# Expert-mixing loop of an encoder block: multiplications by the gate in turn with the value chunks, the gate table in two buffers of 4 chunks instead of one of 8, and the gathered block's work spread to the last chunk

## The chip, the cores and the metric

The kernel runs on one core of a Trainium2 chip. Five engines share the core's on-chip memory: TensorE (PE in the profile, with its weight loads as PEld), VectorE (DVE), ScalarE (ACT), GpSimd (POOL), and SyncE (SP), which here only issues DMAs. Each engine works through its own queue strictly in order and waits on semaphores that other engines or DMAs raise. The metric is the device time of one execution in microseconds (us), median of several runs; lower is better.

## The reference, cut to what matters

One encoder layer over 512 tokens of width 1024 in float32: a mixing part (attention and a gated recurrence), then a PEER layer, then a gated embedding. The part that the change is about is the PEER layer, a retrieval over 16384 experts, each of one neuron:

```python
# ht: 512 tokens; idx, g: for every token 8 heads x 16 chosen experts and their softmax weights
ue = jnp.take(u, ib, axis=0)                    # rows of u of the chosen experts
a = jnp.einsum('thkd,td->thk', ue, xb)
w = jax.nn.gelu(a) * gb
ve = jnp.take(v, ib, axis=0)                    # rows of v
out = jnp.einsum('thk,thkd->td', w, ve)
```

After it come a residual add, an RMSNorm, a product with `ple_gate` under a sigmoid, a product with `p @ ple_proj`, and the last residual add.

## The kernel before, in words

Float32 matrices are split into a high and a low part of a rounded format (`split`: ACT copies the high part, line 139, DVE subtracts to get the low part, line 140), and every product is three matmuls (`mm3`, lines 133 to 136).

The PEER layer is computed in two ways. For tokens 128 to 511 (384 tokens) it is dense: all 16384 experts, in 128 chunks of 128 experts. For each chunk `dense_a` computes gelu(u · h) as a tile `ge` of 128 experts x 384 tokens (24 matmuls of 384 columns into `pa`, gelu on ACT). The weights of the chosen experts stand in a dense table in DRAM, `gdram` (zero where an expert was not chosen), which `build` has written. Later the chunk's `ge` is multiplied by its part of the table, split into `w_h` and `w_l`, and multiplied with the chunk's 128 rows of v (`w_mm`, 18 matmuls of 512 columns into the six accumulators `po`). For tokens 0 to 127 (block 0) it is sparse: GpSimd gathers, by indirect DMA, one row of u per token and slot (`gu`, 128 slots), DVE multiplies and sums it (line 889), then one row of v per slot (`gv`), which DVE adds into `acc` (line 898).

The order of the work: 62 of the 128 chunks have their `ge` computed while the table is still being built, and are spilled to DRAM (`adram`); the other 66 ("fresh") are computed inside the last loop. That loop (line 1014) runs over the 128 chunks; spilled and fresh ones alternate almost one to one (`chunk_order`). In each round `w_prep` does this:

- if the chunk is the first of a group of `GC` = 8, it loads the table for 8 chunks into `gchg` (line 988, 1536 KB, in rows of `GC` x `GB` x 4 = 1024 bytes). There is one such buffer (`B_GC` = 1), so the load waits until the last multiplication of the group before is done;
- it loads the chunk of v (`v_raw`, line 990, 512 KB, 3 buffers) and splits it into `v_h` and `v_l` (4 buffers each);
- for a spilled chunk it loads `ges` (line 996, 192 KB, 4 buffers), for a fresh one it takes the next `ge` (a ring of `PRE` = 8 buffers);
- DVE multiplies `ge` by the table (line 999, "the multiplication"), and the product is split into `w_h` and `w_l`.

Then `next_a` computes further fresh chunks (u is loaded on line 713, split into `u_h`, `u_l`), `w_mm` follows, and `gathers` traces as many gather steps as a pace asks for: the steps on u reach their last slot at round 110 (`IT1` - `UEND`), those on v at round 118 (`IT1`). All DVE steps of the gathers are tied behind the round's multiplication (`issue_after(dve.ins)`). The program is traced in this order, but a scheduler fixes the order of each queue at compile time from priorities and estimated times; `issue_after` adds an edge that it has to keep. So multiplications may stand in DVE's queue well ahead of the v splits of earlier chunks, if their inputs are estimated to be there.

At round 118 the pools of the u side are closed, the residual rows `X` are loaded back, `PJ` = p · ple_proj is computed, `acc` is added to `X[0]` (line 1058), and block 0 is finished as far as its first gate tile (`norm_T1` and `gate(0, 0)`, lines 1086 and 1087). The matmuls of the last 4 chunks (`LASTN`) are kept back and run block by block after the loop (line 1088), so that each block's norm can begin while the next block's matmuls run. Then come the other 15 gate tiles (24 matmuls of 256 columns each) and the output.

Of the kernel before, what the change touches and what calls it, by code (L numbers as in the profile page):

```python
# [27 lines left out]

C_ID, C_IOTA, C_COS, C_SIN, C_RST = 0, 128, 256, 384, 512
C_END = C_RST + 2 * T  # L30
# [4 lines left out]
LASTN = 4  # L35
GC = 8
B_GC = 1
HPU = 300
# [9 lines left out]
NTB = TD // GB  # L48
PRE = 8
SP = 62  # L50
# [8 lines left out]
HPW = 1  # L59
IT1 = 118  # L60
WLAG = 4
VLEAD = 0
# [23 lines left out]
def const_arrays():  # L86
    c = np.zeros((128, C_END), np.float32)
    c[:, C_ID:C_ID + 128] = np.eye(128, dtype=np.float32)
    c[:, C_IOTA:C_IOTA + 128] = np.arange(128, dtype=np.float32)[None]
    t = np.arange(T)  # L90
    row, col = (t // 64).astype(np.float32), (t % 64).astype(np.float32)
    inv = np.float32(10000.0) ** (-np.arange(16, dtype=np.float32) / np.float32(16))
    ang = np.stack([row[:, None] * inv, col[:, None] * inv], axis=1).astype(np.float32)
    for off, fn in ((C_COS, np.cos), (C_SIN, np.sin)):
        c[:, off:off + 128] = fn(ang).astype(np.float32).reshape(NT, 128, 32).transpose(1, 0, 2).reshape(128, 128)
    rst = np.ones((8, 128), np.float32)
    rst[:, 0] = 0.0
    c[:, C_RST:C_END] = rst.reshape(-1)[None]
# [27 lines left out]
def body(nc, tc, I, out, taps=None, stop=99):  # L126
# [17 lines left out]
    with contextlib.ExitStack() as top:  # L144
        glob = top.enter_context(tc.tile_pool(name="glob", bufs=1))
        cst = glob.tile([128, C_END], F32, name="cst")
        ident = cst[:, C_ID:C_ID + 128]
# [48 lines left out]
        if True:  # L196
# [17 lines left out]
            with tc.tile_pool(name="n1", side="right", bufs=1) as n1:  # L214
                ss = n1.tile([128, NT], F32, name="ss1")
                x1 = [n1.tile([128, D], F32, name=f"x1_{tb}") for tb in range(NT)]
                sq = n1.tile([128, D], F32, name="sq1")
                DM.dma_start(x1[0], I["x"][0:128, :])
                DM.dma_start(cst[:, 0:C_COS], I["cst"][:, 0:C_COS])
# [7 lines left out]
                DM.dma_start(cst[:, C_COS:C_END], I["cst"][:, C_COS:C_END])  # L227
# [105 lines left out]
            def hgrn_head(h):  # L333
# [4 lines left out]
                fl = "p a t -> p (a t)"  # L338
                V.tensor_tensor_scan(SC.rearrange(fl), cst[:, C_RST:C_END], LF.rearrange(fl), 0.0, OP.mult, OP.add)
                S4 = SC.rearrange("p a (c j) -> p a c j", c=4)  # L340
# [143 lines left out]
            for tb in range(NT):  # L484
                for (src, dst, H, o, gg) in ((aq[:, tb, :], qr, 8, 0, qn_g), (akv[:, tb, 0:128], kr, 2, 8, kn_g)):
# [7 lines left out]
                    co, si = [cst[:, off + 32 * tb:off + 32 * tb + 32].rearrange("p (a i) -> p a i", a=2)[:, None]  # L493
                              .to_broadcast([128, H, 2, 16]) for off in (C_COS, C_SIN)]
# [157 lines left out]
        h2n = pp.tile([128, D], F32, name="h2n")  # L652
        v8s = [pp.tile([128, 16, 16], F32, name=f"v8_{tb}") for tb in range(NT)]
        i8s = [pp.tile([128, 16, 16], U32, name=f"i8_{tb}") for tb in range(NT)]
        with s5:
# [101 lines left out]
def peer(nc, tc, I, out, xd, cst, gains, norm_T1, rstd_of, split, mm3, tap, stop, pp, ha, la, h2n, v8s, i8s, st, top,  # L757
# [8 lines left out]
    if True:  # L766
# [112 lines left out]
        un, vn = I["peer_u"], I["peer_v"]  # L879

        def gather(src, k, tag):
            t = gt.tile([128, D], F32, name=tag, tag=tag)
# [90 lines left out]
        if stop <= 6:  # L973
            return

        vp = ys.enter_context(tc.tile_pool(name="vstr", side="right", bufs=2, reuse_waits="tile"))
        pso = ys.enter_context(tc.psum_pool(name="pso", side="right", bufs=1, reuse_waits="tile"))
        po = [[pso.tile([128, 512], F32, name=f"po{tc_}{n}") for n in range(2)] for tc_ in range(3)]
        gch = {}
        N0 = na  # L980
        def w_prep(it):
            c = it
            spilled = it in spidx
# [8 lines left out]
            vl = vp.tile([128, D], F32R, name="v_l", tag="v_l", bufs=B_VS)  # L992
            split(vr, vh, vl)
            if spilled:
                ge = vp.tile([128, TD], F32, name="ges", tag="ges", bufs=B_GE)
                DM.dma_start(ge, ad[spidx[c]])
            else:
                ge = pend.pop(0)
            mi = V.tensor_tensor(ge.rearrange("p (b t) -> p b t", t=GB), ge.rearrange("p (b t) -> p b t", t=GB),  # L999
                                 gch[key][:, :, c % GC, :], op=OP.mult)  # L1000
            wh = vp.tile([128, TD], F32R, name="w_h", tag="w_h", bufs=B_W)
# [12 lines left out]
        for it in range(128):  # L1014
# [7 lines left out]
            else:  # L1022
                last.append((it, ops))
            if it < IT1:
                if it >= G0:
                    gathers(GW + (it + 1 - G0) * (128 + WLAG - GW) / (IT1 - UEND - G0), VLEAD + (it + 1 - G0) * 128 / (IT1 - G0), ops[0], ops[5])
            if it == IT1:
                gathers(999, 999, ops[0], ops[5])
                ul_st.close()
# [7 lines left out]
                with tc.tile_pool(name="ple1a", side="left", **LR) as pa:  # L1037
# [7 lines left out]
                    for n in range(2):  # L1045
# [6 lines left out]
                        for tb in range(NT):  # L1052
# [4 lines left out]
                            S.activation(PJ[tb][:, 512 * n:512 * n + 512], pj, AF.Copy)  # L1057
                V.tensor_tensor(X[0], X[0], acc, op=OP.add)
                pe2 = [e1.enter_context(tc.tile_pool(name="ple2", side="left", **LR))]
# [25 lines left out]
                wg0 = load_wg(0)  # L1085
                norm_T1(pe2[0], ps1, "p1", X[0], 2, h3h, h3l, "n3", 0, B_XN)
                gate(0, 0, *wg0, ps1, "p1")
        for tb in range(3):
            for it, ops in last:
                w_mm(it, tb, ops)  # L1090
            for n in range(2):
                xs = X[tb + TB0][:, 512 * n:512 * n + 512]
                V.tensor_tensor(xs, xs, po[tb][n], op=OP.add)
            norm_T1(pe2[0], ps1, "p1", X[tb + TB0], 2, h3h, h3l, "n3", tb + TB0, B_XN)
        ys.close()
        with contextlib.ExitStack() as e2:
            pe2.append(e2.enter_context(tc.tile_pool(name="ple3", side="right", **LR)))
            ps = e2.enter_context(tc.psum_pool(name="psp", side="right", bufs=4, reuse_waits="tile"))
            for n in range(4):
                w = wg0 if n == 0 else load_wg(n)  # L1100
                for tb in range(1 if n == 0 else 0, NT):
                    gate(tb, n, *w, ps, "pg2")
# [58 lines left out]
```

## Time and profile before

| | us |
|---|---|
| median of 3 runs | 1895.51 |
| lowest and highest of them | 1892.5, 1896.64 |
| the profiled execution, as timed | 1892.72 |
| its span, first to last instruction | 1890.9 |
| PE busy | 1811.2 (96%) |
| PE weight loads busy | 1618.7 (86%) |
| DVE busy | 1394.3 (74%) |
| ACT busy | 901.9 (48%) |
| POOL busy | 385.4 (20%) |

The span is what the profile's own clock shows; 1.8 us of the profiled execution lie around it. "PEclk" is the share of full speed that TensorE's clock was granted. In waits, "A <- B: x, n, y" says that engine A's instruction stood idle x us in n times, the longest y us, and B ended that. In groups, "xN | busy, mean ns | idle before" says how many instructions there were, how long they were busy, how long one took on average, and how long the engine had been idle just before them. Busy times of matmuls are modelled ends: a matmul shown with 0.39 us is followed by the next one 0.23 us later.

### The profile page before, as it was taken

The page shows a single profiled execution, that of the slowest core. Times are in us where ns is not written, and L with a number is a line of the kernel's source. Part 1 is how long each engine was busy: PE and PEld are TensorE (multiplying, and loading weights), DVE is VectorE, ACT ScalarE, POOL GpSimd, SP SyncE. Part 2 cuts the span into 40 slices and gives each one's busy share as a digit, 9 for nine tenths or more (in the row PEclk, how much of TensorE's full clock was granted, in tenths as well). Part 3 has the DMA queues.
Part 4 walks back from the last instruction along what each step waited for, and adds up shares of the span by engine and source line. Part 5 has one row for each costly group of instructions (what it writes and reads, how often), then busy time and mean ns, then how long its engine had stood idle before and what let it go on. Part 6 is the DMA issues. An engine that isn't in the chain of part 4 may idle for free.

```text
span 1890.9 us, 27215 instructions
## 1 busy us (share of the span) xinstructions
PE 1811.2 (96%) x9989; PEld 1618.7 (86%) x9989; DVE 1394.3 (74%) x2844; ACT 901.9 (48%) x1561; POOL 385.4 (20%) x260
## 2 busy tenths in 40 slices
PE   6999999999998999998999999999998988999998
PEld 5997887888787999998998888888887877888888
DVE  3689777535798999998656787887877666757464
ACT  5745656532433566975894333333332323333452
POOL 0000000000000222425001345554444333211000
PEclk9999999999999999999999999999999999999999
DMA  4212100333421678888659999999987877776512
GB/s 163 79 46 84 51 12 16 129 102 100 163 83 50 229 260 330 299 291 318 265 201 328 343 352 339 352 334 345 347 300 276 301 267 281 273 250 213 207 59 87
DMA packets 137975, 402.95 MB, mean 213 GB/s; under 512 B 13297, under 2 KB 56049, under 8 KB 136177
## 3 DMA queue, kind: packets, MB, share of 16 engines
q1 hardware_dynamic: 100976, 266.98, 40.3%
q0 software_dynamic: 36864, 134.23, 19.7%
q8 instruction: 78, 1.28, 0.3%
q14 instruction: 57, 0.46, 0.1%
HBM read 359.62 MB, written 41.55 MB: 212 GB/s over the span
## 4 chain that ended last, share of the span: by engine, by line
PE 74%; DVE 13%; DMA 7%; ACT 2%; issue 2%; POOL 0%; SPq 0%; DVEq 0%; ACTq 0%; POOLq 0%
PE po L135 8%; PE po L136 8%; PE po L134 8%; PE pa L136 6%; PE pa L135 6%; PE pa L134 6%; PE pg L872 4%; PE pT L134 3%; PE pT L135 3%; PE pT L136 3%; DMA ges<-adram 3%; DVE u_l L140 2%; PE poa L566 2%; PE pq L134 2%; PE pq L135 2%
## 5 line engine op out<-in xcount | busy, mean ns | idle before, releaser
L883 POOL DMA_INDIRECT gu<-in_peer_u_dram,idxg x128 | 192.6, 1505 | 1117.4 <-DVE cd L808 643.2
L136 PE MATMUL pa<-ha,u_l 128*128 128x384 f32 x1024 | 352.8, 345 | 36.5 <-DVE u_l L140 36.5
L134 PE MATMUL pa<-ha,u_h 128*128 128x384 f32 x1024 | 353.4, 345 | 1.8 <-ACT u_h L139 1.8
L135 PE MATMUL pa<-la,u_h 128*128 128x384 f32 x1024 | 350.1, 342 | 0.0
L135 PE MATMUL po<-v_l,w_h 128*128 128x512 f32 x768 | 300.0, 391 | 0.0
L136 PE MATMUL po<-v_h,w_l 128*128 128x512 f32 x768 | 299.8, 391 | 0.0
L134 PE MATMUL po<-v_h,w_h 128*128 128x512 f32 x768 | 298.9, 389 | 0.3 <-ACT w_h L139 0.3
L883 POOL DMA_INDIRECT gv<-in_peer_v_dram,idxg x128 | 192.6, 1505 | 224.1 <-DVE acc L898 194.8
L136 PEld LDWEIGHTS pa<-ha,u_l 128*128 128x128 f32 x1024 | 196.7, 192 | 42.0 <-DVE u_l L140 41.8
L139 ACT ACTIVATE u_h<-u_raw 128x1024 fp32r<-128x1024 f32 x128 | 135.1, 1055 | 167.0 <-PE pa L135 141.6
L139 ACT ACTIVATE v_h<-v_raw 128x1024 fp32r<-128x1024 f32 x128 | 134.3, 1052 | 144.2 <-DMA v_raw<-in_peer_v_dram 123.0
L134 PEld LDWEIGHTS pa<-ha,u_h 128*128 128x128 f32 x1024 | 197.0, 192 | 5.0 <-ACT u_h L139 2.7
L135 PEld LDWEIGHTS pa<-la,u_h 128*128 128x128 f32 x1024 | 196.6, 192 | 2.3
L140 DVE TENSOR_TENSOR u_l<-u_raw,u_h 128x1024 fp32r<-128x1024 f32 x128 | 155.9, 1218 | 39.6 <-ACT u_h L139 39.6
L136 PEld LDWEIGHTS po<-v_h,w_l 128*128 128x128 f32 x768 | 144.1, 188 | 30.0
L134 PEld LDWEIGHTS po<-v_h,w_h 128*128 128x128 f32 x768 | 144.2, 188 | 29.3 <-ACT w_h L139 0.6
L135 PEld LDWEIGHTS po<-v_l,w_h 128*128 128x128 f32 x768 | 144.1, 188 | 29.1 <-DVE v_l L140 0.3
L140 DVE TENSOR_TENSOR v_l<-v_raw,v_h 128x1024 fp32r<-128x1024 f32 x128 | 155.8, 1218 | 17.0 <-ACT v_h L139 17.0
L889 DVE SCALAR_TENSOR_TENSOR gu<-gu,h2n 128x1024 f32<-128x1024 f32 x128 | 155.1, 1215 | 13.9 <-DMA gu<-in_peer_u_dram,idxg 13.9
L898 DVE SCALAR_TENSOR_TENSOR acc<-gv,aa,acc 128x1024 f32<-128x1024 f32 x128 | 163.7, 1279 | 2.0 <-DMA gv<-in_peer_v_dram,idxg 1.7
L867 ACT ACTIVATE gR<-gE,gr 128x128 f32<-128x128 f32 x384 | 122.1, 393 | 32.8 <-DVE gE L864 32.6
L999 DVE TENSOR_TENSOR ges<-ges,gchg 128x384 f32<-128x384 f32 x62 | 34.0, 554 | 137.3 <-DMA ges<-adram 91.4
(321 smaller groups left out, 3409.8 us busy)
## 6 DMA issues: line engine op xcount, KB each, us to landing
u_raw<-in_u_t_dram SPq DMA_DIRECT2D x128, 512.0 KB
v_raw<-in_peer_v_dram SPq DMA_DIRECT2D x128, 512.0 KB
gdram<-gs SPq DMA_DIRECT2D x12, 2048.0 KB
gchg<-gdram SPq DMA_DIRECT2D x16, 1536.0 KB
w_raw<-in_w_in_dram SPq DMA_DIRECT2D x42, 512.0 KB
adram<-ge SPq DMA_DIRECT2D x62, 192.0 KB
ges<-adram SPq DMA_DIRECT2D x62, 192.0 KB
wq_raw<-in_peer_wq_dram SPq DMA_DIRECT2D x16, 512.0 KB
```

The source lines that it names most:

```text
L134: PE.matmul(ps, lh, rh, start=first, stop=False)
L135: PE.matmul(ps, lh, rl, start=False, stop=False)
L136: PE.matmul(ps, ll, rh, start=False, stop=last)
L139: ins = S.activation(hi, raw, AF.Copy)
L140: V.tensor_tensor(lo, raw, hi.bitcast(F32), op=OP.subtract)
L566: PE.matmul(po, PTs[g][:, s * 128:(s + 1) * 128], akv[:, s, 128 + 64 * g:192 + 64 * g], start=(s == 0), stop=(s == 3))
L867: S.activation(RR[:, t, :], EE[:, 1, t, :], AF.Copy, scale=gr[:, t0 + t:t0 + t + 1])
L872: PE.matmul(pg[:, :, w], RR[:, t, :], EE[:, 0, t, :], start=True, stop=True)
L883: G.indirect_dma_start(out=t, out_offset=None, in_=src, in_offset=bass.IndirectOffsetOnAxis(ap=idxg[:, k:k + 1], axis=0))
L889: V.scalar_tensor_tensor(t, t, 1.0, h2n, op0=OP.mult, op1=OP.mult, accum_out=aa[:, k:k + 1])
L898: V.scalar_tensor_tensor(acc, t, aa[:, k:k + 1], acc, op0=OP.mult, op1=OP.add)
L999: mi = V.tensor_tensor(ge.rearrange("p (b t) -> p b t", t=GB), ge.rearrange("p (b t) -> p b t", t=GB), gch[key][:, :, c % GC, :], op=OP.mult)
```

## The change

- **In turn.** The multiplication of a chunk is tied on DVE behind the previous chunk's `v_l` subtraction (`issue_after(vi[-2].ins)`).
- **Table.** `GC` = 4 and `B_GC` = 2: the table is read for 4 chunks at a time into one of two buffers, 32 loads of 768 KB in rows of 512 bytes.
- **Spilled tiles.** The load of `ges` is traced at the head of `w_prep`, ahead of the table and of `v_raw`, instead of behind the split of v.
- **Gathers.** The u steps are paced to round 118 instead of 110, the v steps to round 128 instead of 118. `gv` gets a pool of its own on the other side of the memory, so that its buffers outlive round 118.
- **Block 0.** The addition of `acc`, the norm of block 0 and a first gate tile come after the matmuls, the addition and the norm of the loop's first dense block; that gate tile is block 1's instead of block 0's.
- **Memory.** `PRE` 7 instead of 8; tables of cosines and the scan's reset move from a lasting tile to one of the front pool; the top-8 lists move to a pool that is freed at round 118.

```diff
-GC = 8
-B_GC = 1
+GC = 4
+B_GC = 2
-PRE = 8
+PRE = 7
+VEND = 128
+GLEAD = 0
...
+        gpool["gv"] = ys.enter_context(tc.tile_pool(name="gathv", side="right", bufs=B_G, reuse_waits="tile"))
...
         def w_prep(it):
+            nonlocal nb
+            while nb < min(128, it + 1 + GLEAD):
+                if nb in spidx:
+                    back[nb] = vp.tile([128, TD], F32, name="ges", tag="ges", bufs=B_GE)
+                    DM.dma_start(back[nb], ad[spidx[nb]])
+                nb += 1
...
-            split(vr, vh, vl)
+            S.activation(vh, vr, AF.Copy)
+            vi.append(V.tensor_tensor(vl, vr, vh.bitcast(F32), op=OP.subtract))
             if spilled:
-                ge = vp.tile([128, TD], F32, name="ges", tag="ges", bufs=B_GE)
-                DM.dma_start(ge, ad[spidx[c]])
+                ge = back.pop(c)
             else:
                 ge = pend.pop(0)
-            mi = V.tensor_tensor(ge.rearrange("p (b t) -> p b t", t=GB), ge.rearrange("p (b t) -> p b t", t=GB),
-                                 gch[key][:, :, c % GC, :], op=OP.mult)
+            with tc.issue_after(vi[-2].ins) if len(vi) > 1 else contextlib.nullcontext():
+                mi = V.tensor_tensor(ge.rearrange("p (b t) -> p b t", t=GB), ge.rearrange("p (b t) -> p b t", t=GB),
+                                     gch[key][:, :, c % GC, :], op=OP.mult)
...
-            if it < IT1:
-                if it >= G0:
-                    gathers(GW + (it + 1 - G0) * (128 + WLAG - GW) / (IT1 - UEND - G0), VLEAD + (it + 1 - G0) * 128 / (IT1 - G0), ops[0], ops[5])
+            if it >= G0:
+                gathers(999 if it >= IT1 else GW + (it + 1 - G0) * (128 + WLAG - GW) / (IT1 - G0), (it + 1 - G0) * 128 / (VEND - G0), ops[0], ops[5])
             if it == IT1:
-                gathers(999, 999, ops[0], ops[5])
...
-                V.tensor_tensor(X[0], X[0], acc, op=OP.add)
...
-                norm_T1(pe2[0], ps1, "p1", X[0], 2, h3h, h3l, "n3", 0, B_XN)
-                gate(0, 0, *wg0, ps1, "p1")
...
             norm_T1(pe2[0], ps1, "p1", X[tb + TB0], 2, h3h, h3l, "n3", tb + TB0, B_XN)
+            if tb == 0:
+                gathers(999, 999)
+                V.tensor_tensor(X[0], X[0], acc, op=OP.add)
+                norm_T1(pe2[0], ps1, "p1", X[0], 2, h3h, h3l, "n3", 0, B_XN)
+                gate(TB0, 0, *wg0, ps1, "p1")
...
-                for tb in range(1 if n == 0 else 0, NT):
+                for tb in (0, 2, 3) if n == 0 else range(NT):
```

More of the change, by code (lines that the diff above doesn't have):

```diff
@@ L27 @@
 NCELL = sum(ROW_N)
-C_ID, C_IOTA, C_COS, C_SIN, C_RST = 0, 128, 256, 384, 512
+C_ID, C_IOTA, C_FR = 0, 128, 256
+C_COS, C_SIN, C_RST = 0, 128, 256
 C_END = C_RST + 2 * T
@@ L86, in const_arrays @@
 def const_arrays():
-    c = np.zeros((128, C_END), np.float32)
+    c = np.zeros((128, C_FR + C_END), np.float32)
     c[:, C_ID:C_ID + 128] = np.eye(128, dtype=np.float32)
@@ L94, in const_arrays @@
     for off, fn in ((C_COS, np.cos), (C_SIN, np.sin)):
-        c[:, off:off + 128] = fn(ang).astype(np.float32).reshape(NT, 128, 32).transpose(1, 0, 2).reshape(128, 128)
+        c[:, C_FR + off:C_FR + off + 128] = fn(ang).astype(np.float32).reshape(NT, 128, 32).transpose(1, 0, 2).reshape(128, 128)
     rst = np.ones((8, 128), np.float32)
     rst[:, 0] = 0.0
-    c[:, C_RST:C_END] = rst.reshape(-1)[None]
+    c[:, C_FR + C_RST:] = rst.reshape(-1)[None]
     s = np.arange(128)
@@ L145, in body @@
         glob = top.enter_context(tc.tile_pool(name="glob", bufs=1))
-        cst = glob.tile([128, C_END], F32, name="cst")
+        cst = glob.tile([128, C_FR], F32, name="cst")
         ident = cst[:, C_ID:C_ID + 128]
@@ L201, in body @@
             hT_l = fp.tile([128, ND, T], F32R, name="hT_l")
+            cfr = fp.tile([128, C_END], F32, name="cfr")
             ysp = [[fp.tile([128, 4, T], F32R, name=f"{nm}{p}") for p in "hl"] for nm in "oy"]
@@ L218, in body @@
                 DM.dma_start(x1[0], I["x"][0:128, :])
-                DM.dma_start(cst[:, 0:C_COS], I["cst"][:, 0:C_COS])
+                DM.dma_start(cst, I["cst"][:, 0:C_FR])
                 DM.dma_start(gains, I["gains"])
@@ L226, in body @@
                 pre[1280] = wtile(w_in[10], (8, 128))
-                DM.dma_start(cst[:, C_COS:C_END], I["cst"][:, C_COS:C_END])
+                DM.dma_start(cfr, I["cst"][:, C_FR:C_FR + C_END])
                 r = rstd_of(n1, ss, NT, 1.0 / D, "n1")
@@ L338, in hgrn_head @@
                 fl = "p a t -> p (a t)"
-                V.tensor_tensor_scan(SC.rearrange(fl), cst[:, C_RST:C_END], LF.rearrange(fl), 0.0, OP.mult, OP.add)
+                V.tensor_tensor_scan(SC.rearrange(fl), cfr[:, C_RST:C_END], LF.rearrange(fl), 0.0, OP.mult, OP.add)
                 S4 = SC.rearrange("p a (c j) -> p a c j", c=4)
@@ L492, in body @@
                     x1, x2 = s5[:, :, :, 0, :], s5[:, :, :, 1, :]
-                    co, si = [cst[:, off + 32 * tb:off + 32 * tb + 32].rearrange("p (a i) -> p a i", a=2)[:, None]
+                    co, si = [cfr[:, off + 32 * tb:off + 32 * tb + 32].rearrange("p (a i) -> p a i", a=2)[:, None]
                               .to_broadcast([128, H, 2, 16]) for off in (C_COS, C_SIN)]
@@ L652, in body @@
         h2n = pp.tile([128, D], F32, name="h2n")
-        v8s = [pp.tile([128, 16, 16], F32, name=f"v8_{tb}") for tb in range(NT)]
-        i8s = [pp.tile([128, 16, 16], U32, name=f"i8_{tb}") for tb in range(NT)]
         with s5:
@@ L705, in body @@
             ul_st = contextlib.ExitStack()
+            tp = ul_st.enter_context(tc.tile_pool(name="top8", side="left", **LR))
+            v8s = [tp.tile([128, 16, 16], F32, name=f"v8_{tb}") for tb in range(NT)]
+            i8s = [tp.tile([128, 16, 16], U32, name=f"i8_{tb}") for tb in range(NT)]
             up = [ul_st.enter_context(tc.tile_pool(name="ustr0", side="left", **LR))]
@@ L879, in peer @@
         un, vn = I["peer_u"], I["peer_v"]
+        gpool = {"gu": gt}
         def gather(src, k, tag):
-            t = gt.tile([128, D], F32, name=tag, tag=tag)
+            t = gpool[tag].tile([128, D], F32, name=tag, tag=tag)
             G.indirect_dma_start(out=t, out_offset=None, in_=src,
@@ L979, in peer @@
         gch = {}
+        vi = []
         N0 = na
+        back = {}
+        nb = 0
         def w_prep(it):
+            nonlocal nb
[4 more added lines that the diff above has]
+                nb += 1
             c = it
```

## The prediction

> **What bounds the kernel now.** I read the page first: TensorE is busy nearly all the time, so only what keeps it from working, or slows it, can be gained.
>
> ```profile
> span 1890.9 us, 27215 instructions
> PE 1811.2 (96%) x9989; PEld 1618.7 (86%) x9989; DVE 1394.3 (74%) x2844; ACT 901.9 (48%) x1561; POOL 385.4 (20%) x260
> ```
>
> Next I cut the last loop (about 1000 to 1830 us) into stretches. Columns: length, then busy time and instructions of PE, PEld, DVE, ACT, POOL, then granted clock, share of the DMA engines, GB/s.
>
> ```profile
> 1000.00:1390.00 390.00, 389.71 (x1895) 344.69 (x1894) 307.35 (x397) 144.49 (x208) 169.53 (x112) 1.00 0.93 339
> 1390.00:1720.00 330.00, 306.89 (x1440) 271.27 (x1439) 222.05 (x278) 105.40 (x148) 109.52 (x74) 0.96 0.78 276
> 1720.00:1800.00 80.00, 80.00 (x376) 68.97 (x375) 45.67 (x62) 32.06 (x45) 4.83 (x4) 1.00 0.60 203
> 1800.00:1891.00 91.00, 84.64 (x562) 76.68 (x560) 51.24 (x122) 35.05 (x72) 0.00 (x0) 1.00 0.23 76
> ```
>
> In the first and third stretch TensorE never stops and has its full clock. In the second it is idle for 23.1 us (330 - 306.89) and its mean clock is 0.96. DVE is busier and the DMA engines are fuller in the first stretch than in the second, so the loss is not a lack of either. PE's waits in the two stretches (first row: 1000 to 1390; second: 1390 to 1720) name the culprit:
>
> ```profile
> PE po L134 <- ACT w_h L139: 0.3, 1, 0.3
> PE pa L136 <- DVE u_l L140: 23.1, 8, 5.0
> ```
>
> All 23.1 us are eight waits for `u_l`, the low part of a chunk of u. The first of them, on PE and on DVE:
>
> ```profile
> 1448.47 0.34 PE L135 MATMUL pa<-la,u_h 128*128 128x384 f32 x1
> 1453.78 0.62 PE L136 MATMUL pa<-ha,u_l 128*128 128x384 f32 x1 [4.97 <-DVE u_l L140]
> ```
>
> ```profile
> 1444.30 1.21 DVE L140 TENSOR_TENSOR v_l<-v_raw,v_h 128x1024 fp32r<-128x1024 f32 x1
> 1450.88 0.56 DVE L999 TENSOR_TENSOR ges<-ges,gchg 128x384 f32<-128x384 f32 x1 [5.37 <-DMA ges<-adram]
> 1451.36 1.22 DVE L889 SCALAR_TENSOR_TENSOR gu<-gu,h2n 128x1024 f32<-128x1024 f32 x1
> 1452.50 0.08 DVE L889 DVE_READ_ACCUMULATOR gu<-gu,h2n 128x1 f32 x1
> 1452.50 1.22 DVE L140 TENSOR_TENSOR u_l<-u_raw,u_h 128x1024 fp32r<-128x1024 f32 x1
> ```
>
> DVE stood 5.37 us at a multiplication whose spilled tile had not landed, and the `u_l` that PE needed was queued behind it. Was that multiplication due? Counting multiplications (first two rows) and `v_l` subtractions (DVE column of the last two rows) from 1000 us on answers:
>
> ```profile
> 1000.00:1200.00 200.00, 19.91 (x37) 1.00 0.94 340
> 1000.00:1600.00 600.00, 53.48 (x98) 0.98 0.89 322
> 1000.00:1200.00 200.00, 77.04 (x198) 37.16 (x198) 43.80 (x36) 1.00 0.94 340
> 1000.00:1600.00 600.00, 210.98 (x540) 101.33 (x540) 109.48 (x90) 0.98 0.89 322
> ```
>
> At 1200 us DVE has done 37 multiplications and 36 `v_l`; at 1600 us 98 and 90. So the multiplications have drifted 8 chunks ahead of the v splits. A chunk takes 390 / 63 = 6.2 us (63 `v_l` stand in the first stretch, row below), so they come some 50 us before they are needed, and wait for inputs that are only just requested. DVE's waits from 1390 to 1720 (three rows) and from 1000 to 1390 (last row):
>
> ```profile
> DVE ges L999 <- DMA ges<-adram: 77.7, 18, 9.2
> DVE ge L999 <- DMA gchg<-gdram: 22.8, 3, 10.6
> DVE ges L999 <- DMA gchg<-gdram: 6.5, 1, 6.5
> DVE ges L999 <- DMA gchg<-gdram: 39.3, 6, 8.9
> ```
>
> The table costs DVE about as much in the first stretch (39.3 us) as in the second (29.3 us), without any loss on PE. What is new in the second is 77.7 us for spilled tiles, that is, the drift.
>
> **The change part by part.**
>
> *In turn.* The multiplication of chunk c now stands behind the `v_l` of chunk c - 1. The drift cannot form, and DVE is where it was at 1200 us, where PE lost nothing. This gives back the idle 23.1 us and the clock: 0.04 x 330 = 13.2 us (11.6 to 14.9 by the rounding of 0.96). Sum -36.3 us. What is late next? Between 1000 and 1390 nothing was, at a fuller load; I leave 1 us for what remains. Queued behind the waiting multiplication are the round's gather steps, `w_l` and later `u_l`; those who wait for them (GpSimd's buffers, PE) are served in turn as well.
>
> *The load on DVE in turn.* Groups of the first stretch:
>
> ```profile
> L898 DVE SCALAR_TENSOR_TENSOR acc<-gv,aa,acc 128x1024 f32<-128x1024 f32 x69 | 88.1, 1277 | 1.7 <-DMA gv<-in_peer_v_dram,idxg 1.7
> L140 DVE TENSOR_TENSOR v_l<-v_raw,v_h 128x1024 fp32r<-128x1024 f32 x63 | 76.6, 1218 | 13.3 <-ACT v_h L139 13.3
> L889 DVE SCALAR_TENSOR_TENSOR gu<-gu,h2n 128x1024 f32<-128x1024 f32 x44 | 53.5, 1216 | 0.0
> L999 DVE TENSOR_TENSOR ge<-ge,gchg 128x384 f32<-128x384 f32 x35 | 19.0, 549 | 5.5 <-DMA gchg<-gdram 5.5
> L889 DVE SCALAR_TENSOR_TENSOR gu<-gu,h2n 128x1024 f32<-128x1024 f32 x26 | 31.6, 1217 | 0.0
> ```
>
> (The last row is of the second stretch.) Per chunk DVE does `v_l` 1.22, the multiplication 0.55, `w_l` of the same size 0.55, and `u_l` 66/128 x 1.22 = 0.63. The gathers: 128 v steps over 120 rounds at 1.28 make 1.36; the 44 + 26 = 70 u steps that the loop still has, over 110 rounds at 1.22 + 0.08, make 0.83. That is 5.1 us of 6.2, with 1.1 us per chunk to spare. The first stretch did 113 gather steps in 63 chunks, 1.8 per chunk; the new pace asks 1.7. So spreading them costs nothing as long as that spare time holds; without it, the price is the third rival's.
>
> *Table in two buffers.* The load of a group no longer waits for the multiplication just before. SP issues it in order behind the previous `v_raw`, which waits for the `v_l` three chunks before it, so about three chunks (18 us) ahead of use; the longest wait for a whole 1536 KB table was 10.6 us. The table's waits go, worth nothing on PE beside the first item. The price is on the DMA engines: 32 x 1536 = 49152 rows of 512 bytes instead of 24576 of 1024. The trace of before shows no such load; I bound a row from two stretches of the DMA queues, the first (10 us long) mostly table rows, the second (1100 to 1390) mostly gathered rows:
>
> ```profile
> q1 hardware_dynamic: 1521, 1.73, 50.0%
> q0 software_dynamic: 13162, 47.90, 44.5%
> ```
>
> A packet took 0.500 x 160 / 1521 = 52.6 ns at 1137 bytes, and 0.445 x 290 x 16 / 13162 = 157 ns at 3639 bytes: 5 ns plus 0.042 ns per byte. Rows of 512 and 1024 bytes then take 26.5 and 47.8 ns, and the change adds (49152 x 26.5 - 24576 x 47.8) / 16 = 8 us to each DMA engine over the loop. The ends are 0 (only bytes count) and 73 us (half a row costs as much as a whole one). I take 8, since the two rows give so small a constant. The loop's DMA work is 0.93 x 390 + 0.78 x 330 + 0.60 x 80 = 668 us; with 8 more over 800 - 35 = 765 us that is a share of 0.88, under the 0.93 at which PE lost nothing. Cost 0.
>
> The Trainium skill, page "DMA: Bandwidth & Descriptors", section "Bandwidth", speaks against this part: batch DMAs to 1 MiB or more, and (section "Anatomy of one DMA — SWDGE (gpsimd) path") reckon about 2.0 us fixed per DMA. By that rule 16 more loads would be an estimated 32 us more in the queue, and the sum would be about zero if none of it overlapped. No wait of this trace is such a fixed cost, as the queue carries other loads meanwhile; hence my small weight on it.
>
> *Spilled tiles first.* Their load is issued earlier in a round and no longer behind the table; a gain for DVE only, 0 on PE.
>
> *`PRE` 7.* Counting produced against consumed fresh chunks in the code, at most 7 are alive, and only from round 95 on. A gelu then waits for the `w_l` of the same or the previous round, which PE needs at that time as well: 0, with 5 us as the far end if ACT's queue is held.
>
> *Block 0 late.* The last v step now stands behind the multiplication of chunk 127. The matmuls removed from round 118 and added at the end are the same, so PE's work stays; what grows is the chain of DVE in the tail. Rows from 1795 to 1850:
>
> ```profile
> L1093 DVE TENSOR_TENSOR x<-x,po 128x512 f32<-128x512 f32 x6 | 4.1, 685 | 2.4 <-PE po L136 2.4
> L190 DVE SCALAR_TENSOR_TENSOR la<-pt_n,gains,ha 128x128 fp32r<-128x128 f32 x25 | 7.8, 344 | 1.3 <-ACT ha L189 1.3
> L179 DVE TENSOR_SCALAR xn_n<-x,rr_n 128x1024 f32<-128x1024 f32 x4 | 3.0, 749 | 0.1
> L162 DVE SCALAR_TENSOR_TENSOR rq_n<-rr_n,rm_n 128x1 f32<-128x1 f32 x8 | 1.7, 218 | 0.3
> L184 PE MATMUL pt_n<-cst,xn_n 128*128 128x128 f32 x32 | 4.5, 279 | 1.5 <-DVE xn_n L179 1.2 <-DVE la L190 0.3
> ```
>
> ```profile
> 1447.62 0.39 PE L134 MATMUL po<-v_h,w_h 128*128 128x512 f32 x1
> 1447.85 0.39 PE L135 MATMUL po<-v_l,w_h 128*128 128x512 f32 x1
> ```
>
> Block 0 adds an addition (2 x 0.69), 8 x 0.34 for `la`, 0.75 for `xn` and ten tiny steps of about 0.2: some 7 us among three other blocks. PE has work to cover it: 8 transposes (4.5 / 4 = 1.1 us) and one more gate tile, 24 matmuls of 256 columns at half the 0.23 us from one matmul of 512 to the next (2.8 us), 4 us together. I take the difference, +3, between 0 and 7.
>
> *The front and the moved tables.* The same loads at the same places; 0, give or take 3 us for a schedule that comes out differently.
>
> **Sum.** -36.3 + 1 + 3 = -32 us: the profiled span goes from 1890.9 to about 1859, its time from 1892.7 to 1860.6. The profiled execution is at the low end of the runs; the median is 2.8 us above, so I forecast 1895.5 - 32 = 1863.5 us. Own range 1855 to 1872 (tail 0 to 7, `PRE` 5, front 3).
>
> **The rivals.**
>
> 1. *Half of it.* The order of a queue is fixed by estimates, and other early steps (gathers, gelus) may hold `u_l` instead. For: 13.3 us of DVE's waits in the first stretch are on ACT. Against: PE lost nothing there. Half of 36 us stays: 1863.5 + 18 = 1881. Chance 0.13.
> 2. *No change: the DMA engines become the bound.* If a row of 512 bytes costs as much as one of 1024, the loop's DMA work is 668 + 73 = 741 us; at the share of 0.93 that takes 797 of today's 800 us, and the gain is gone: about 1893. It decides from about 40 ns per row on. Against: the small constant above. Chance 0.06. The rule of the Trainium skill on small DMAs (same page) would act here.
> 3. *Slower: multiplications in turn wait for their table.* With no drift a late table holds `v_l`, `w_l` and `u_l` at once. If a load comes as late as now, 32 loads at 39.3 / 6 = 6.6 us make 210 us of waits; DVE has 128 x 1.1 = 141 us to spare, so 69 us come on top of the sum: about 1932. It decides if the issue leads the multiplication by less than the roughly 10 us of a load. Against: the lead of three chunks, 15 us even if DVE runs at its own 5.1 us per chunk. Chance 0.07.
>
> **How the numbers follow.** About 0.2% (4 us) is what a measurement of this kernel can tell from no change. The forecast has 0.74; rival 1 gives 0.13, faster too; rival 2 is "same", 0.06; rival 3 "slower", 0.07. So faster 0.87, same 0.06, slower 0.07. Range: 1852 (if the tail's present gaps close as well) to 1882, which takes in most of rival 1 and leaves out rivals 2 and 3.
>
> **What would show it.** Right: PE's waits for `u_l` after 1390 us gone and the granted clock 1.00 throughout the loop; as many multiplications as `v_l` at any time; DVE's waits for `gchg` near zero; a DMA share near 0.9 until the end of the loop; PE's tail gaps a few us longer. Wrong: new PE waits on `po` for `w_h` or `v_l` (rival 3), a DMA share of 0.95 or more with late `v_raw` (rival 2), `u_l` late behind gather steps (rival 1).

## The result and the profile after

The changed kernel takes 1862.64 us (median of 4 runs, 1856.46 to 1863.68); the kernel before, run beside it, 1894.01 us (1890.86 to 1896.64). The ratio is 0.9828, with a 95% interval of 0.9801 to 0.9856: faster by 1.7%, at 1863.5 us forecast. The profiled execution took 1861.94 us. Medians are of fast runs; one run of an experiment below (d1_lead5, 1988.92 us at a granted clock of 0.85) was slow and is left out.

The page of the kernel after, span and engines:

```profile
span 1860.1 us, 27252 instructions
PE 1804.9 (97%) x9989; PEld 1613.2 (87%) x9989; DVE 1401.1 (75%) x2844; ACT 902.3 (49%) x1561; POOL 349.9 (19%) x260
```

The number of matmuls is the same (x9989). The span is 30.8 us shorter: PE is busy 6.3 us less (1811.2 - 1804.9) and idle 24.5 us less (79.7 - 55.2). To see where, the kernel after by stages (columns as in the prediction: length, busy and instructions of PE, PEld, DVE, ACT, POOL, clock, DMA share, GB/s):

```profile
0.00:1000.00 1000.00, 957.86 (x5755) 864.49 (x5756) 768.56 (x1990) 585.69 (x1091) 96.85 (x70) 0.99 0.46 157
1000.00:1720.00 720.00, 717.26 (x3481) 634.57 (x3480) 545.56 (x681) 261.68 (x370) 242.00 (x182) 1.00 0.91 314
...
1000.00:1390.00 390.00, 387.26 (x1870) 341.38 (x1869) 300.21 (x382) 145.84 (x207) 136.94 (x102) 1.00 0.94 326
1390.00:1720.00 330.00, 330.00 (x1613) 293.19 (x1612) 245.35 (x299) 115.84 (x164) 105.05 (x80) 1.00 0.88 298
1720.00:1800.00 80.00, 75.39 (x335) 62.44 (x334) 54.38 (x84) 33.02 (x49) 11.07 (x8) 0.98 0.58 204
```

and the same two long stages of the kernel before:

```profile
0.00:1000.00 1000.00, 950.00 (x5723) 857.13 (x5724) 768.00 (x1989) 584.91 (x1089) 101.58 (x70) 0.99 0.45 157
1000.00:1720.00 720.00, 696.60 (x3333) 615.96 (x3332) 529.40 (x674) 249.89 (x356) 279.04 (x186) 0.98 0.86 310
```

The second stretch, with 23.1 us of idle time and a clock of 0.96 before, is now full: PE 330.00 of 330 us at 1.00. As busy time depends on the clock, the matmuls done are the better measure of progress. Between 1000 and 1720 us PE did 3481 instead of 3333, 148 more. Where PE hardly stops, a matmul takes 720 / 3499 = 0.206 us (3499 of them in 720 us in the experiment with the tie alone, row below), so the loop won 148 x 0.206 = 30.5 us. At 1000 us PE was already 32 matmuls ahead, about 5.6 us at that stage's 1000 / 5723 = 0.175 us. The rest of the span gave back 30.5 + 5.6 - 30.8 = some 5 us.

What PE waits for in the kernel after, from 1000 to 1390 us (first row) and from 1390 to the end (the others):

```profile
PE po L137 <- ACT v_h L1011: 2.7, 1, 2.7
...
PE pjp L137 <- ACT pj L1074: 4.3, 1, 4.3
PE pg L137 <- ACT ha L192: 1.1, 2, 0.9
```

The eight waits for `u_l` are gone. Two new stops are there, one at the start of the loop and one, 4.3 us, at `PJ` (about 1751 to 1755 us). The drift, counted as in the prediction: multiplications (first two rows) and `v_l` (DVE column of the last two):

```profile
1000.00:1200.00 200.00, 20.34 (x37) 0.99 0.96 335
1000.00:1600.00 600.00, 54.54 (x99) 1.00 0.93 321
1000.00:1200.00 200.00, 77.36 (x198) 37.30 (x198) 43.98 (x36) 0.99 0.96 335
1000.00:1600.00 600.00, 220.47 (x565) 106.17 (x565) 119.84 (x98) 1.00 0.93 321
```

99 against 98 at 1600 us, where it was 98 against 90: the two kinds now go in step. DVE's waits for inputs of the multiplication between 1000 and 1720 us have shrunk to one line:

```profile
DVE ges L1018 <- DMA gchg<-gdram: 2.8, 1, 2.8
```

### The profile page after: what moved, and what is told of

Its sections match the earlier page's. It is cut to its first block, busy times and chain, and to the rows that moved or that the text cites. A ratio compares the mean times of both kernels' runs of the same rounds, so it can differ in the third digit from the quotient of the medians.

```text
span 1860.1 us, 27252 instructions
## 1 busy us (share of the span) xinstructions
PE 1804.9 (97%) x9989; PEld 1613.2 (87%) x9989; DVE 1401.1 (75%) x2844; ACT 902.3 (49%) x1561; POOL 349.9 (19%) x260
## 3 DMA queue, kind: packets, MB, share of 16 engines
q8 instruction: 78, 1.28, 0.3%
## 4 chain that ended last, share of the span: by engine, by line
PE 79%; DVE 10%; DMA 5%; ACT 3%; issue 2%; SPq 0%; POOL 0%; ACTq 0%; DVEq 0%; POOLq 0%
PE po L137 9%; PE po L138 9%; PE po L139 9%; PE pa L139 6%; PE pa L138 6%; PE pa L137 6%; PE pg L877 3%; PE pT L138 3%; PE pT L137 3%; PE pT L139 3%; DMA gdram<-gs 2%; PE poa L570 2%; PE pq L137 2%; PE pq L138 2%; PE pq L139 2%
## 5 line engine op out<-in xcount | busy, mean ns | idle before, releaser
L139 PE MATMUL pa<-ha,u_l 128*128 128x384 f32 x1024 | 347.6, 339 | 6.1 <-DVE u_l L143 6.1
L137 PE MATMUL pa<-ha,u_h 128*128 128x384 f32 x1024 | 348.4, 340 | 0.3 <-ACT u_h L142 0.3
L890 POOL DMA_INDIRECT gv<-in_peer_v_dram,idxg x128 | 155.7, 1216 | 317.6 <-DVE acc L905 214.9
L869 DVE TENSOR_TENSOR gE<-cst,tij 128x2048 f32<-128x2048 f32 x48 | 109.3, 2287 | 18.4 <-PE pg L877 18.4
```

The lines of the kernel that those rows point to most:

```text
L137: PE.matmul(ps, lh, rh, start=first, stop=False)
L139: PE.matmul(ps, ll, rh, start=False, stop=last)
L869: V.tensor_tensor(EE, iota[:, None, None, :].to_broadcast([128, 2, TQ, 128]), tij[:, :, t0:t0 + TQ, None].to_broadcast([128, 2, TQ, 128]), ...
L890: G.indirect_dma_start(out=t, out_offset=None, in_=src, in_offset=bass.IndirectOffsetOnAxis(ap=idxg[:, k:k + 1], axis=0))
```

## The experiments

The theory to be tested (A): the whole gain is the order; a multiplication that DVE's queue holds chunks too early waits for its data, and `u_l` stands behind it. The tie cures this, the new table is worth nothing on PE. The rival (B): the table in two buffers brings a good part, as multiplications stop waiting for it. Later runs ask how far the order may drift, what a late table costs, and what makes the two new stops. All twelve, each beside runs of the kernel before:

| run | base and edit | median us | ratio, 95% interval | span us |
|---|---|---|---|---|
| a1_turn_only | before + tie | 1859.25 | 0.9818 (0.9790 to 0.9847) | 1857.1 |
| a2_table_only | before + two tables of 4 | 1956.30 | 1.0338 (1.0298 to 1.0378) | 1952.0 |
| a3_no_turn | after - tie | 1942.59 | 1.0263 (1.0217 to 1.0310) | 1943.3 |
| a4_single_table | after, one table of 8 | 1865.64 | 0.9850 (0.9824 to 0.9876) | 1860.5 |
| b1_pace_back | after, gathers at the old pace | 1858.47 | 0.9816 (0.9794 to 0.9837) | 1856.7 |
| b2_turn_and_table | before + tie + two tables of 4 | 1858.23 | 0.9822 (0.9800 to 0.9844) | 1856.4 |
| c1_pj_first | after, `PJ` copies first | 1861.38 | 0.9835 (0.9813 to 0.9857) | 1858.5 |
| e1_turn_pre7 | before + tie, `PRE` 7 | 1862.79 | 0.9838 (0.9815 to 0.9861) | 1860.7 |
| d1_lead5 | before + tie five chunks back | 1860.31 | 0.9814 (0.9782 to 0.9847) | 1858.2 |
| d2_lead5_table | the same + two tables of 4 | 1871.98 | 0.9886 (0.9866 to 0.9907) | 1872.2 |
| f1_turn_one_table4 | before + tie, one table of 4 | 1893.82 | 1.0004 (0.9989 to 1.0019) | 1886.6 |
| b4_rows256 | before + tie, four tables of 2 | 1862.42 | 0.9843 (0.9825 to 0.9860) | 1856.6 |

Spans are of the one profiled execution of each. Five medians missed the range that was written down for them: a1_turn_only came 4 us under that of theory A, a2_table_only and a3_no_turn far above every range, f1_turn_one_table4 4 us above its own, and b4_rows256 lies 4.2 us from b2_turn_and_table where at most 4 was expected.

**The tie alone (a1_turn_only).**

```diff
+        vi = []
-            split(vr, vh, vl)
+            S.activation(vh, vr, AF.Copy)
+            vi.append(V.tensor_tensor(vl, vr, vh.bitcast(F32), op=OP.subtract))
+            with tc.issue_after(vi[-2].ins) if len(vi) > 1 else contextlib.nullcontext():
                 mi = V.tensor_tensor(...)
```

> The kernel before with one edit: each multiplication stands on DVE behind the previous chunk's v_l; one table buffer of 8 chunks, old pace of the gathers, block 0 early. Theory A (the drift of the multiplications ahead of the v splits made the loss): PE's waits for u_l after 1390 us go, as many multiplications as v_l at any time; the table still costs DVE some 5 to 10 us for each of its 16 loads, within its spare time; 1863 to 1872 us. Theory B (the single table buffer made the loss, since each load has to wait for the last multiplication of the group before): the table's waits stay and PE still waits for DVE; 1883 to 1895 us.

Stages of this kernel:

```profile
0.00:1000.00 1000.00, 951.69 (x5721) 857.59 (x5722) 767.99 (x1989) 586.40 (x1089) 101.88 (x70) 0.99 0.45 157
1000.00:1720.00 720.00, 718.81 (x3499) 636.53 (x3498) 551.47 (x691) 259.99 (x371) 274.38 (x190) 1.00 0.89 318
```

It was as far as the kernel before at 1000 us (5721 matmuls against 5723) and did 166 more until 1720 us: 166 x 0.206 = 34.2 us, and the whole span is 33.8 us shorter. The tie alone brings the whole gain. What PE and DVE wait for between 1000 and 1720 us:

```profile
PE po L134 <- ACT w_h L139: 0.9, 1, 0.9
PE po L136 <- DVE w_l L140: 0.3, 1, 0.3
```

```profile
DVE ge L1002 <- DMA gchg<-gdram: 38.9, 7, 9.0
DVE ges L1002 <- DMA gchg<-gdram: 36.4, 7, 8.9
```

The one table still makes DVE wait 75 us, as much as in the kernel before (45.8 + 28.3 = 74 us over the same stretch), and PE loses 1.2 us. Theory A.

**The table alone (a2_table_only).**

```diff
-GC = 8
-B_GC = 1
+GC = 4
+B_GC = 2
```

> The kernel before with one edit: the table in two buffers of 4 chunks, nothing in turn. Theory A: the multiplications drift ahead as before and wait for spilled tiles instead (77.7 us of DVE's waits in the second stretch were those); PE keeps most of its 23 us of waits for u_l; 1883 to 1895 us. Theory B: the table's waits are gone and PE's with them; 1862 to 1870 us.

Slower by 63 us, which neither theory had expected. PE's waits from 1000 to 1720 us, and DVE's in the whole loop:

```profile
PE pa L136 <- DVE u_l L140: 48.3, 16, 6.1
PE po L134 <- ACT w_h L139: 10.6, 2, 10.4
PE po L135 <- DVE v_l L140: 4.5, 5, 2.0
```

```profile
DVE ges L999 <- DMA ges<-adram: 133.0, 29, 9.7
DVE ges L999 <- DMA gchg<-gdram: 77.1, 10, 8.7
DVE ges L999 <- issue: 24.2, 5, 5.7
```

The second buffer did not take the table's waits away (77.1 us against 74 in the kernel before). 90 multiplications against 82 `v_l` are done at 1600 us, the drift of 8 chunks of the kernel before. But the count isn't the whole of it: at 1200 us it is only 33 against 31, and PE has lost 26 of the first 390 us (363.73 us busy), where the kernel before lost 0.3 (389.71). The last row is idle time with no releaser in the profile, at the same multiplications. What these waits cost is compared under f1_turn_one_table4; one stop has a place of its own, the 10.4 us at about 1067 us (see d2_lead5_table). Why two tables without the tie do worse than one is open beyond that.

**The changed kernel without the tie (a3_no_turn).**

```diff
-            with tc.issue_after(vi[-2].ins) if len(vi) > 1 else contextlib.nullcontext():
+            with contextlib.nullcontext():
```

> The changed kernel without the tie of the multiplication behind the previous v_l, all else as changed. Theory A: the drift is back (multiplications 5 chunks or more ahead of v_l by 1600 us), with DVE's waits for spilled tiles and PE's for u_l; 1878 to 1895 us. Theory B: as the changed kernel, 1858 to 1867 us.

80 us slower than with the tie, in the expected direction and further than expected. PE waits 47.1 us for `u_l` again, DVE 106.3 us for `ges`, 80.4 us for the table; at 1600 us 92 multiplications stand against 86 `v_l`. None of the change's other parts replaces the tie, and with two tables it matters more than without.

**The changed kernel with one table of 8 (a4_single_table).** `GC` 4 -> 8, `B_GC` 2 -> 1.

> The changed kernel with the table in one buffer of 8 chunks again, all else as changed. Theory A: DVE waits for the table 5 to 10 us at each of 16 loads, PE hardly at all; 1862 to 1872 us. Theory B: PE's waits are back; 1880 to 1895 us.

1865.64 us, within what can be told from the changed kernel (the intervals overlap). The table's waits on DVE return, and PE's stops stay at 3.5 us in the loop and 5.7 us at `PJ`. Theory B falls.

**Gathers at the old pace (b1_pace_back).** Block 0 stays late; u steps until round 110, v steps until 118:

```diff
-VEND = 128
+VEND = 118
-   gathers(... GW + (it + 1 - G0) * (128 + WLAG - GW) / (IT1 - G0), ...
+   gathers(... GW + (it + 1 - G0) * (128 + WLAG - GW) / (IT1 - UEND - G0), ...
```

> The changed kernel with the old pace of the gathers: u steps done at round 110, v steps at round 118; block 0 still finishes late. If the wider spread matters for TensorE, DVE's spare time of some 1 us per chunk shrinks to about 0.7 and PE waits in the first 700 us of the loop, 1866 us or more. If it is covered (the prediction's view), no PE wait appears before round 118, and with lighter gathers at the end the 4.3 us that PE now stands at the products of PJ near 1750 us become smaller: 1858 to 1863 us.

The stop at `PJ` is gone and the span 3.4 us shorter; the 2.7 us at the start of the loop stay. The DMA share rose to 0.96 in the first stretch, with no new PE wait above 0.8 us. The timeline of the kernel after shows what the later gathers do at `PJ`. ACT (start, us; in brackets the idle time before, and what ended it):

```profile
1733.26 1.06 ACT L142 ACTIVATE ph<-pr 128x1024 fp32r<-128x1024 f32 x1 [8.83 <-DMA pr<-in_pT_dram]
...
1746.62 0.53 ACT L142 ACTIVATE w_h<-ges 128x384 fp32r<-128x384 f32 x1 [1.80 <-DVE ges L1018]
1749.98 0.53 ACT L142 ACTIVATE w_h<-ge 128x384 fp32r<-128x384 f32 x1 [2.83 <-DVE ge L1018]
1750.41 1.04 ACT L1011 ACTIVATE v_h<-v_raw 128x1024 fp32r<-128x1024 f32 x1
1753.35 0.52 ACT L142 ACTIVATE w_h<-ges 128x384 fp32r<-128x384 f32 x1 [1.90 <-DVE ges L1018]
1753.78 1.04 ACT L1011 ACTIVATE v_h<-v_raw 128x1024 fp32r<-128x1024 f32 x1
1754.72 1.06 ACT L1074 ACTIVATE pj<-pjp 128x512 f32<-128x512 f32 x2
```

and DVE in the same time:

```profile
1734.35 1.23 DVE L143 TENSOR_TENSOR pl<-pr,ph 128x1024 fp32r<-128x1024 f32 x1 [10.44 <-ACT ph L142]
...
1746.04 0.55 DVE L1018 TENSOR_TENSOR ges<-ges,gchg 128x384 f32<-128x384 f32 x1
1746.51 1.28 DVE L905 SCALAR_TENSOR_TENSOR acc<-gv,aa,acc 128x1024 f32<-128x1024 f32 x1
1747.70 1.22 DVE L1012 TENSOR_TENSOR v_l<-v_raw,v_h 128x1024 fp32r<-128x1024 f32 x1
1748.84 0.55 DVE L143 TENSOR_TENSOR w_l<-ges,w_h 128x384 fp32r<-128x384 f32 x1
1749.31 0.56 DVE L1018 TENSOR_TENSOR ge<-ge,gchg 128x384 f32<-128x384 f32 x1
1749.77 1.28 DVE L905 SCALAR_TENSOR_TENSOR acc<-gv,aa,acc 128x1024 f32<-128x1024 f32 x1
```

DVE stands 10.44 us at the split of p, whose load is late, and has to catch up without a gap. But every round now holds a gather step of 1.28 us ahead of the next `v_l`, so multiplications come some 3.3 us apart with no time to spare (in b1_pace_back, without gather steps, DVE waits some 1.1 us for ACT in each such round). ACT waits for each of them at `w_h`, and the copy that frees PE's accumulator for `PJ` stands behind two `w_h`. PE, with only two such accumulators, stops.

**`PJ` copies first (c1_pj_first).** A higher priority (`tc.high_priority`) around the copy of line 1074.

> The changed kernel with one edit: the copies of PJ from the accumulators on ACT get a higher priority, so that they are not queued behind splits of w that wait for multiplications. If that queue position makes PE's 4.3 us stop near 1750 us, the stop and the half clock after it go (some 6 us): 1855 to 1858 us. If PE stops there because DVE is behind, it stays or moves: 1861 to 1864 us.

The stop stays, 3.7 us against 4.3. But the priority did not move the copy: it still stands behind two `w_h` (1748.19 and 1751.56 us, the copy at 1752.94), each of which waits for a multiplication. So the run doesn't tell whether the copy's place in ACT's queue or DVE's lateness decides; the timelines show the two together. The late load of p (8.2 us on ACT here, 4.1 in b1_pace_back) and the gather steps after it were not taken apart; with gather steps and a wait of 4.6 us (a4_single_table) the stop is there, with 4.1 us and no gather steps it isn't, which speaks for the steps.

**The tie and the table on the kernel before (b2_turn_and_table).** Both edits above, nothing else.

> The kernel before with two edits: in turn, and the table in two buffers of 4 chunks; old pace, block 0 early, 8 buffers for fresh tiles, spilled tiles loaded where they were. If the table's two buffers add something once the multiplications are in turn, DVE's waits for the table (75 us with one buffer) go and the time falls below that of in turn alone (1859): 1855 to 1858 us. If DVE's waits were hidden anyway, the same 1859 us within 3.

1858.23 us against 1859.25 with the tie alone. DVE's table waits fall from 75 to 0.9 us, and the time doesn't move: the clearest sight of a wait that costs nothing. The tie alone is thus the simplest version that has the gain; the span here is 3.7 us under the changed kernel's, though the medians' intervals overlap.

**`PRE` 7 beside the tie (e1_turn_pre7).** a1_turn_only with `PRE` 8 -> 7.

> The kernel before with two edits: in turn, and 7 buffers for fresh tiles instead of 8. The prediction put this at 0 with 5 us as the far end. If the seventh tile is the last that PE can compute before the loop's first v has been split, PE stops some 3 us at about 1005 us as in the changed kernel, 1862 to 1864 us; if not, 1859 us as with in turn alone.

No stop at the start of the loop (PE's longest wait in the loop is 1.4 us), so `PRE` 7 isn't its cause. The loop does 3501 matmuls until 1720 us, as with `PRE` 8 (3499); the 3.6 us of span more were lost before 1000 us, where 17 matmuls are missing. That isn't `PRE` either: with 8 buffers d1_lead5 stands at 5706 matmuls there, e1_turn_pre7 at 5704. The median fell into the range that was expected with a stop, but its interval overlaps that of a1_turn_only. The 2.7 us stop (2.7 to 3.5) is in all kernels made from the changed one and in none made from the kernel before. ACT in the kernel after shows what holds it:

```profile
1006.23 0.52 ACT L142 ACTIVATE w_h<-ges 128x384 fp32r<-128x384 f32 x1 [4.30 <-DVE ges L1018]
1006.86 1.06 ACT L1011 ACTIVATE v_h<-v_raw 128x1024 fp32r<-128x1024 f32 x1
```

The first `v_h`, which PE needs, stands behind a `w_h` that waits for a multiplication, which waited 2.8 us for the table; in b2_turn_and_table the first `v_h` (1010.27 us) stands ahead of `w_h` (1012.18 us). PE also begins the loop's products 4.8 us earlier here (1007.97 against 1012.74 us). `gv`'s own pool, the spilled tiles first and the moved tables are left as what set this order, and were not taken apart. `PRE` 8 in the changed kernel wasn't tried.

**How much lead is harmless (d1_lead5).** a1_turn_only with the tie to the `v_l` five chunks back instead of one:

```diff
-            with tc.issue_after(vi[-2].ins) if len(vi) > 1 ...
+            with tc.issue_after(vi[-6].ins) if len(vi) > 5 ...
```

> The kernel before with a looser tie: each multiplication stands behind the v_l of the chunk five before it, so it may run up to five chunks (31 us) ahead; one table buffer of 8. Theory A, refined: a lead costs only when it reaches the ring of four spilled tiles (some 8 chunks), because then every spilled tile is loaded only after a w_l that stands behind the waiting multiplication. With five chunks PE's loss stays small: 1859 to 1868 us. If any lead beyond a chunk or two already makes DVE wait for inputs, 1875 us or more.

```profile
1000.00:1390.00 390.00, 390.00 (x1899) 345.52 (x1899) 310.52 (x398) 144.86 (x209) 173.28 (x113) 1.00 0.94 341
1390.00:1720.00 330.00, 330.00 (x1612) 293.17 (x1611) 245.20 (x299) 115.99 (x164) 107.02 (x77) 1.00 0.84 297
```

PE is busy in all of the 720 us, with 77 us of table waits on DVE as before. The order need not be strict. It has to be kept from drifting so far that the multiplications outrun the loads: spilled tiles have four buffers and every second chunk is a spilled one, so by the code their loads can lead by some eight chunks. Where the harm begins was not measured closer: the lead here is 5 at 1500 and 1600 us, without loss; in the kernel before it was 6 at 1400 and 1500 us, when the waits for spilled tiles set in (4.3 us before 1390 us, 77.7 after), and 8 at 1600.

**Lead and two tables (d2_lead5_table).** d1_lead5 with `GC` 4, `B_GC` 2.

> The kernel before with the same looser tie (five chunks) and the table in two buffers of 4 chunks. If two small tables were harmful without the tie (1956 us) because the multiplications also ran ahead of what two buffers of 4 hold, a lead of five chunks still asks for the third group while the first is in use: some loss of PE, 1865 to 1900 us. If the harm came from the spilled tiles alone: as with the looser tie and one table.

14 us longer in the span than with one table. PE has one stop for it:

```profile
PE po L134 <- ACT w_h L139: 10.8, 2, 10.3
```

It lies at some 1068 to 1078 us. The multiplication that PE needs (chunk 12) starts at 1077.4 us, after those of chunks 13, 15, 17 and 19, behind DVE's waits of 6.65 and 3.38 us for gathered rows. With a table at hand for later chunks the compile-time order can put their multiplications first; that this is why is an argument, the order itself is in the trace. a2_table_only has the same stop (10.4 us); a tie to the chunk before forbids it.

**The third rival brought about (f1_turn_one_table4).** The tie, with one table of 4: each load is half as long, but is issued only when the last multiplication of the group before is done, so the lead is gone.

> In turn, and the table in one buffer of 4 chunks: 32 loads, each issued only when the last multiplication of the group before is done. This is the third rival of the prediction on purpose. DVE's waits for the table come to 32 x 5 us or more = 160 us against the 141 us that it has to spare: PE stops again by a few tens of us in all, 1865 to 1890 us. If DVE's spare time is larger than reckoned, 1858 to 1862 us.

1893.82 us, ratio 1.0004 (0.9989 to 1.0019): all of the gain is gone. (The profiled execution, 1888.47 us, was the fastest of ten.) DVE's waits at multiplications in the whole loop, and PE's from 1000 to 1720 us:

```profile
DVE ges L1002 <- DMA gchg<-gdram: 110.7, 17, 9.6
DVE ge L1002 <- DMA gchg<-gdram: 69.5, 11, 8.3
DVE ges L1002 <- DMA v_raw<-in_peer_v_dram: 8.2, 1, 8.2
```

```profile
PE pa L136 <- DVE u_l L140: 14.9, 7, 3.6
PE po L134 <- ACT w_h L139: 4.2, 1, 4.2
PE po L136 <- DVE w_l L140: 0.9, 1, 0.9
```

The prediction gave DVE 141 us to spare in the loop. Kernels that differ in the tie and the table alone, with all of DVE's waits for inputs of multiplications over the loop, against the span with the tie alone:

| kernel | waits, us | above 141, us | span over a1_turn_only, us |
|---|---|---|---|
| b2_turn_and_table | 3 | none | -0.7 |
| b4_rows256 | 3 | none | -0.5 |
| d2_lead5_table | 53 | none | 15.1 |
| a1_turn_only | 75 | none | 0 |
| d1_lead5 | 78 | none | 1.1 |
| before | 166 | 25 | 33.8 |
| f1_turn_one_table4 | 190 | 49 | 29.5 |
| a2_table_only | 235 | 94 | 94.9 |

Up to 78 us such waits are free, unless one of them, or the order itself, makes a stop of its own (d2_lead5_table); from 166 us on the time goes up. That 141 is the border isn't shown: nothing between 78 and 166 was run, and where PE hardly stops, DVE has more to spare than reckoned. In b2_turn_and_table it is idle 720 - 556.7 = 163 us of the 720 (PE busy 719.3), 1.4 us per chunk of 6.2, some 180 us for 128 chunks. The kernel before lost its 33.8 us below that. What the total leaves out is where the waits stand: 107 of its 166 us lie in one stretch of 330 us, in which 1.4 x 330 / 6.2 = 75 us were to spare.

**Rows of 256 bytes (b4_rows256).** b2_turn_and_table with `GC` 2, `B_GC` 4: 64 loads of 384 KB.

> In turn, and the table in four buffers of 2 chunks: 64 loads of 384 KB in rows of 256 bytes (98304 rows). By 5 ns plus 0.042 ns per byte a row takes 16 ns and each DMA engine gets 98304 x 16 / 16 = 98 us of table rows, 16 more than with 512 bytes; the share from 1000 to 1390 us rises from 0.96 to about 0.98 and the time stays within 4 us of in turn with two buffers of 4 (1858). If the second rival of the prediction holds (a row's cost hardly falls with its size), the DMA engines are full, v_raw comes late and the time is 1880 us or more.

```profile
1000.00:1390.00 390.00, 387.68 (x1881) 342.13 (x1880) 310.80 (x395) 146.01 (x208) 146.10 (x110) 1.00 1.01 336
...
q1 hardware_dynamic: 50260, 51.94, 55.3%
```

The second row is the queue of SP's loads from 1100 to 1390 us (packets, MB, share of 16 engines). The same row with rows of 512 bytes (b2_turn_and_table) and with 1024 (a1_turn_only):

```profile
q1 hardware_dynamic: 31938, 50.67, 50.9%
```

```profile
q1 hardware_dynamic: 22825, 51.44, 48.9%
```

Twice halved rows raise the share by 2.0 and 4.4 points at about equal bytes (50.67 to 51.94 MB): (0.509 - 0.489) x 290 x 16 / 9113 = 10 ns for each packet more, then (0.553 - 0.509) x 290 x 16 / 18322 = 11 ns. From the first to the last it is (0.553 - 0.489) x 290 x 16 / 27435 = 11 ns. The DMA engines come to a share of 1.01 (a sum of packet times, which can pass 1) where 0.98 was expected, and PE loses 2.3 us of 390, 2.0 of it in one wait for `w_h`.

## Why the prediction was right

**In turn, -36.3 + 1.** Right in mechanism and nearly in size: the tie alone won 34.2 us in the loop against 35.3 forecast, by the two signs that were named (no waits for `u_l`, clock 1.00). In the whole change the loop won 30.5 us; the residue was not 1 us but about 6 (36.3 - 30.5): most of it is the stop of 2.7 us at its start with the slower clock after it (0.99 in the row to 1200 us, 2 us), which some part other than the tie brings.

**The load on DVE.** That there is time to spare is borne out (75 us of waits are free, 190 cost 30, 235 cost 95); its size was put too low, 1.1 us per chunk against 1.4 in b2_turn_and_table, and 141 us is not shown to be a border (table under f1_turn_one_table4).

**Table, 0.** Right in the sum, as two tables beside the tie change nothing (b2_turn_and_table). Wrong in two steps that the sum didn't feel. A packet's constant was put at 5 ns and measured 10 to 11, so the load added an estimated 24576 x 10.5 / 16 = 16 us to each DMA engine, not 8. And a share of 0.93 was taken as the bound at which PE is proven to lose nothing; at 0.96 PE lost 0.7 us of 390 (b2_turn_and_table), at 1.01 2.3 us. The second rival would have needed far more. The rule of the Trainium skill (page "DMA: Bandwidth & Descriptors", sections "Bandwidth" and "Anatomy of one DMA — SWDGE (gpsimd) path"), to batch to 1 MiB and to count 2.0 us for each load, which the page gives for DMAs that GpSimd issues and the prediction applied to loads that SP issues, isn't a price here: 16, 32 and 64 loads gave 1859, 1858 and 1862 us. What agrees is another rule of the same page (section "Rules for kernel authors"), that the fixed cost overlaps where a load is issued early and waited for late: DVE's table waits fell to 0.9 us with two tables and rose to 180 us where the lead was taken away (f1_turn_one_table4).

**What the table does without the tie** was not seen: the prediction treated the parts as independent, and on its own this part costs 63 us.

**Gathers, 0, and block 0 late, +3.** The tail lost about 5 us, near the forecast by the wrong term. The chain of block 0's norm cost nothing: in the last 90.9 us PE does 561 matmuls and is idle 6.0 us (90.9 - 84.89, row below), where the kernel before did 562 and was idle 6.3 (90.9 - 84.64). The loss is the stop at `PJ`, 4.3 us and 1.6 us of clock (0.02 x 80). It comes from the spread of the gathers, which was costed at nothing: with the old pace alone put back the stop is gone and the span 3.4 us shorter (b1_pace_back). The spare time was worked out for the loop's mean round, and at round 118 DVE has a 10 us wait to make good in rounds of 3.3 us.

```profile
1769.20:1860.10 90.90, 84.89 (x561) 76.74 (x559) 58.87 (x140) 36.05 (x74) 0.00 (x0) 1.00 0.23 76
```

**`PRE` 7, 0.** No stop came of it (e1_turn_pre7).

**The front, 0 give or take 3.** The 32 matmuls gained before 1000 us, some 5.6 us, lie past that margin. All kernels made from the changed one have them (5753 to 5770 matmuls at 1000 us) and none made from the kernel before (5702 to 5731), so some part of the rest of the change brings them; which, is open. They made good what the two stops cost: forecast were 35.3 + 0 - 3 us, measured 30.5 + 5.6 - 5.3. That the sum came out within 1 us is luck; that the tie is the gain is not.

**The rivals.** Half of it: nothing else held `u_l`. No change by the DMA engines: fallen (b4_rows256). Multiplications waiting for their table: the mechanism is real (f1_turn_one_table4), and the lead that two buffers give keeps it off here; with one table of 8 the 75 us of waits stayed free as well (a1_turn_only).

## What to carry to other kernels

Count two kinds of instruction that belong to the same step over time in one engine's queue: where one count runs away from the other, an early step stands in front of a late one, and its wait is paid by whoever is queued behind; a tie that caps the lead cures it (here a cap of one chunk or, with one table, of five). Add up what an engine has to spare in a stage before paying for a shorter wait on it: here 75 us of waits spread over the loop cost nothing, and 166 us, most of them in one stretch, cost 34 us. Try the parts of a change alone: here one part carried all of the gain, and another, without it, would have cost nearly twice that gain.

## What the runs showed of the hardware

The 16 DMA engines can show a share of 0.96 to 1.01 over 390 us while TensorE loses at most 3.8 us (b1_pace_back 386.19 us busy, b4_rows256 387.68 us). A packet more on the queue of SP's loads, at about the same bytes, went with 10 to 11 ns more of one DMA engine's time (22825, 31938 and 50260 packets). And two table buffers of 4 chunks in place of one of 8, with nothing else changed, made the kernel 63 us slower (a2_table_only); beside the tie they made no difference (b2_turn_and_table).
